# Attention weights kept by key block and multiplied with V once per pair of heads; the memory transposed early, its split parts where the tokens' features were

## The chip, the cores and the metric

The kernel runs on one core of a Trainium2 chip. The metric is the device time of one execution in microseconds (us), the median of several runs. The engines have short names: PE is the matrix engine (PEld its weight loads), DVE the vector engine, ACT the scalar engine, POOL GpSimd, SP the engine whose queue issues most transfers. Each engine works through its own instructions in order.

## The reference

One decoder layer on 512 tokens of 1024 features. What the change touches is the first part, two kinds of attention with 8 heads of 64 features each, and the keys and values of 256 memory tokens:

```
u = rmsnorm(h)
[qA|kA|vA|qB|kB|vB|fA] = u @ w_in
oA = forgetting attention over heads A: softmax(q.k/8 + decay), causal, times v
oB = stick-breaking attention over heads B: exp(log_sigmoid(z) + tail sums), strictly causal, times v
h  = h + concat(rmsnorm(oA), rmsnorm(oB)) @ w_out
h  = h + cross_attention(rmsnorm(h) -> rmsnorm(mem))
h  = h + experts(rmsnorm(h))
out = rmsnorm(h)
```

## The kernel before

All matrix work is in 32-bit floats. Large products are made of three products of split parts (`mm3`, L134): a high part (name ending in `h`) and a rest (ending in `l`), both in the format float32r. A weight unit of 1024 values a partition is loaded by SP (`wload`), copied to its high part by ACT (L89), and its rest is made by DVE (L90). The attention products with V and the transposes are plain float32.

Phase 1 handles the heads in pairs, p = 0 to 3, with one pair of each kind at a time. `qk_proj` makes the queries and keys of a pair (PE rows `pj<-uh,wh`, 512 columns each) and SP copies them into tiles `QQ`, `KH`, `KL`, `QX`, `KX`. `sb_pair` and `fox_pair` are generators that work through three sets of query blocks, BLOCKS = (0), (1, 3), (2), first one head and then the other: products into a PSUM tile (`Z` for stick-breaking, two buffers; `lg` for forgetting attention, one), a chain on DVE and ACT that ends in weights, the transposes of these (`transposed`, L319, rows `tr<-ident,sa` and `tr<-ident,p`), and a copy of the transposes to a tile `pT` (six buffers; by ACT for stick-breaking, by DVE for forgetting attention). When both heads of a set have their `pT`, `av` (L312) multiplies it with V: for each query block i and each key block s from i on, one product of 128 columns for each head. The heads' 64 features go to the upper and the lower half of the partitions of one PSUM tile `o4`, which is to say to two halves of the matrix engine's columns; in the trace each product is two records, 320 for 160 products. `pair_out` (L345) copies a finished `o4` to HO (ACT, L346), squares it (ACT, L351) and adds the squares up (DVE, L352).

The generators run in turn ("sfsf..."). The order in which the instructions then stand on each engine is made when the kernel is built, by a scheduler that moves independent work between them: PE gets the next pair's projections (`pj<-uh`), the values' projections (`pj<-wh,uh`), and in pair 3 the memory's keys (`pj<-mh,wh`) as filling between the steps of the attention.

Before pair 0 the memory is normalised and transposed, and each transpose is split at once by ACT and DVE into `mh` and `ml` (`to_fm`, L131, tiles that live beside the tokens' features `uh` and `ul`). After pair 3 come the rest of the memory's keys and values (rows `pj<-mh,wh`, `pj<-wh,mh`, `lg<-wh,mh`) and then the out projection (first row `pja<-wh,fmh`).

Of the kernel before, what the change touches and what calls it, by code (L numbers as in the profile page):

```python
# [21 lines left out]
S = 512  # L22
D = 1024
NT = 4
# [11 lines left out]
FIRST = 4  # L36


def layer(ctx, tc, a, out, dbg=None):
# [100 lines left out]
    # -------------------------------------------------------------- constants  # L140
# [17 lines left out]
    # ================================================= phase 1: projection, FoX, SB  # L158
# [11 lines left out]
    tuneg = pc.tile([128, 512], F32, name="tuneg")  # L170
    nc.gpsimd.memset(tuneg, -1.0)
    affine(tuneg[:, 384:], [[-1, 128]], OP.is_ge, 0.0, 0, 1)
    one2 = pc.tile([2, S], F32, name="one2")
    nc.gpsimd.memset(one2, 1.0)
# [11 lines left out]
    mp = pool(ckm, "mp", side="left")  # L186
    mh = mp.tile([128, KT, M], F32R, name="mh")
    ml = mp.tile([128, KT, M], F32R, name="ml")
# [13 lines left out]
    # ---- forget gates  # L202
# [20 lines left out]
    # ---- pieces  # L223
# [41 lines left out]
    def qk_proj(g, p):  # L265
# [18 lines left out]
        for hh in range(2):  # L284
# [8 lines left out]
            else:  # L293
# [3 lines left out]
                parts += [(QX, 0, qh[P, :]), (QX, 64, one2), (KX, 0, kl[P, :]),  # L297
# [8 lines left out]
    # what the heads give, by feature: the heads of a pair share a tile  # L306
# [3 lines left out]
    # the tokens come last first: the keys of a query block are its own block and those behind it;  # L310
    # the products of a pair's heads run side by side in the columns of the tensor engine
    def av(o, i, at, pTs, vcol):  # L312
        for s in range(i, NT):
            for hh in range(2):
                nc.tensor.matmul(o[hh * HD:(hh + 1) * HD, i * 128:(i + 1) * 128],  # L315
                                 V[:, s, vcol + hh * HD:vcol + (hh + 1) * HD], pTs[hh][:, at + s - i, :],
                                 start=s == i, stop=s == NT - 1)

    def transposed(p, w, copy):  # L319
        pt = trp.tile([128, NT, 128], F32, name="tr")  # L320
        for s in range(w // 128):
            nc.tensor.transpose(pt[:, s, :], p[:, s * 128:(s + 1) * 128], ident)  # L322
        pT = wk.tile([128, NT, 128], F32, name="pT", bufs=6)
        copy(pT[:, :w // 128, :], pt[:, :w // 128, :])
        return pT

    # blocks of queries that are handled together
# [16 lines left out]
    # the features of a pair of heads go to their place; their squares are summed over the pairs  # L344
    def pair_out(o, g, p):  # L345
# [3 lines left out]
        else:  # L349
            s2 = wk.tile([128, S], F32, name="sa", bufs=5)  # L350
# [3 lines left out]
    def fox_pair(p, ops):  # L354
        o = op_.tile([128, S], F32, name="o4", bufs=2)
        for blocks in BLOCKS:
            at, w = spans(blocks)
            pTs = []
            for Q, K in ops:
# [15 lines left out]
                pTs.append(transposed(p_, w, nc.vector.tensor_copy))  # L375
                if len(pTs) == 1:
                    yield
            for i, cs in at:
                av(o, i, cs.start // 128, pTs, p * 128)
            yield  # L380
        pair_out(o, 0, p)
# [4 lines left out]
    def sb_pair(p, ops):  # L386
        o = op_.tile([128, S], F32, name="o4", bufs=2)
        for blocks in BLOCKS:
            at, w = spans(blocks)
            pTs = []  # L390
            for Q, K in ops:
# [4 lines left out]
                e = wk.tile([128, S], F32, name="sa", bufs=5)  # L396
# [4 lines left out]
                c = wk.tile([128, S], F32, name="sa", bufs=5)  # L401
# [4 lines left out]
                if len(pTs) == 1:  # L406
                    yield
# [60 lines left out]
    for p in range(4):  # L468
# [5 lines left out]
        for c in "sf":  # L474
            for _ in steps[c]:
                pass
# [850 lines left out]
```

## Time and profile before

| | |
|---|---|
| time, median of 3 runs (lowest, highest) | 663.63 us (662.79, 664.0) |
| span of the profiled execution | 662.1 us |
| PE busy, share of the span | 625.6 us, 94% |
| DVE, ACT, POOL busy | 461.6, 376.7, 53.1 us |
| moved by DMA | 128.91 MB, 195 GB/s on average |

The span is the time from the first to the last instruction of the profiled execution; it is 1.5 us below the median. A matmul's duration in the trace includes its way through the array, some 0.17 us in which the next one already runs: what one costs is read from the distance between two starts. Rows by stretch give the stretch and its length, then the busy time (and number of instructions) of PE, PEld, DVE, ACT and POOL, the granted clock of PE as a share of full speed, the share of the DMA engines' time, and GB/s. Rows in order of time give start, duration, engine, line, operation, names and shapes. The trace gives the attention of the four pairs from 68.66 us (the first `Z` product) to 260.07 us (the row behind the last product with V).

### The profile page before, as it was taken

The page shows a single profiled execution, that of the slowest core. Times are in us where ns is not written, and L with a number is a line of the kernel's source. Part 1 is how long each engine was busy: PE and PEld are TensorE (multiplying, and loading weights), DVE is VectorE, ACT ScalarE, POOL GpSimd, SP SyncE. Part 2 cuts the span into 40 slices and gives each one's busy share as a digit, 9 for nine tenths or more (in the row PEclk, how much of TensorE's full clock was granted, in tenths as well). Part 3 has the DMA queues.
Part 4 walks back from the last instruction along what each step waited for, and adds up shares of the span by engine and source line. Part 5 has one row for each costly group of instructions (what it writes and reads, how often), then busy time and mean ns, then how long its engine had stood idle before and what let it go on. Part 6 is the DMA issues. An engine that isn't in the chain of part 4 may idle for free.

```text
span 662.1 us, 10336 instructions
## 1 busy us (share of the span) xinstructions
PE 625.6 (94%) x3595; PEld 507.4 (77%) x3596; DVE 461.6 (70%) x941; ACT 376.7 (57%) x752; POOL 53.1 (8%) x80
## 2 busy tenths in 40 slices
PE   3999999999999999999999999999999999999980
PEld 2988777888877888988888898867767777777750
DVE  4843794963497797855853466347879999989955
ACT  5632556653456676613632354333369898898842
POOL 2000000000000000000000003000152011010350
PEclk9999999999999999999999999999999999999996
DMA  8545744323764634561453223792989999999494
GB/s 279 171 125 133 186 113 116 92 65 92 171 157 107 169 104 152 200 218 35 121 166 96 77 84 88 260 367 99 313 258 366 378 388 380 386 383 385 130 201 174
DMA packets 105497, 128.91 MB, mean 195 GB/s; under 512 B 8456, under 2 KB 82240, under 8 KB 105440
## 3 DMA queue, kind: packets, MB, share of 16 engines
q1 hardware_dynamic: 101120, 114.43, 54.8%
q0 software_dynamic: 4320, 13.77, 7.6%
q8 instruction: 29, 0.48, 0.3%
q14 instruction: 28, 0.23, 0.1%
HBM read 103.96 MB, written 11.56 MB: 174 GB/s over the span
## 4 chain that ended last, share of the span: by engine, by line
PE 82%; DMA 6%; DVE 4%; ACT 3%; issue 2%; POOL 1%; SPq 1%; DVEq 0%; POOLq 0%
PE pj L136 8%; PE pj L138 8%; PE pj L137 8%; PE o L315 5%; PE gu L136 4%; PE pja L136 4%; PE gu L137 4%; PE gu L138 4%; PE pja L137 4%; PE pja L138 4%; PE tr L322 3%; PE tr L129 3%; PE pjb L137 3%; PE pjb L136 3%; PE pjb L138 3%; PE dn L136 2%
## 5 line engine op out<-in xcount | busy, mean ns | idle before, releaser
L90 DVE TENSOR_TENSOR wl<-w,wh 128x1024 fp32r<-128x1024 f32 (+1 forms) x64 | 78.3, 1223 | 81.3 <-ACT wh L89 75.1
L89 ACT CAST wh<-w 128x1024 fp32r<-128x1024 f32 (+1 forms) x64 | 67.2, 1050 | 104.5 <-PE pj L137 37.3
L709 DVE TENSOR_TENSOR wl<-w,wh 128x512 fp32r<-128x512 f32 x168 | 108.5, 686 | 5.5 <-ACT wh L708 5.1
L708 ACT CAST wh<-w 128x512 fp32r<-128x512 f32 x168 | 96.6, 621 | 12.8 <-PE gu L138 9.8
L136 PE MATMUL pj<-uh,wh 128*128 128x512 f32 x128 | 52.1, 407 | 0.0
L138 PE MATMUL pj<-uh,wl 128*128 128x512 f32 x128 | 51.5, 403 | 0.0
L137 PE MATMUL pj<-ul,wh 128*128 128x512 f32 x128 | 51.2, 400 | 0.0
L136 PE MATMUL gu<-wh,xh 128*128 128x512 f32 x120 | 48.5, 404 | 0.2 <-ACT xh L131 0.2
L138 PE MATMUL gu<-wh,xl 128*128 128x512 f32 x120 | 47.6, 397 | 0.0
L137 PE MATMUL gu<-wl,xh 128*128 128x512 f32 x120 | 47.1, 393 | 0.0
L136 PE MATMUL pj<-wh,uh 128*128 128x256 f32 (+1 forms) x128 | 37.7, 294 | 2.3 <-ACT uh L131 2.3
L138 PE MATMUL pj<-wh,ul 128*128 128x256 f32 (+1 forms) x128 | 37.5, 293 | 0.0
L137 PE MATMUL pj<-wl,uh 128*128 128x256 f32 (+1 forms) x128 | 37.3, 292 | 0.0
L315 PE MATMUL o<-pT,V 128*64 128x128 f32 x320 | 33.0, 284 | 0.1
L136 PE MATMUL pja<-wh,fmh 128*128 128x512 f32 x80 | 32.4, 405 | 0.0
L137 PE MATMUL pja<-wl,fmh 128*128 128x512 f32 x80 | 31.9, 399 | 0.0
L138 PE MATMUL pja<-wh,fml 128*128 128x512 f32 x80 | 31.8, 398 | 0.0
L315 PEld LDWEIGHTS o<-pT,V 128*64 128x64 f32 x320 | 21.4, 136 | 10.0 <-issue 5.2
L136 PEld LDWEIGHTS pj<-uh,wh 128*128 128x128 f32 x128 | 24.1, 188 | 6.3 <-issue 1.7
L138 PEld LDWEIGHTS pj<-uh,wl 128*128 128x128 f32 x128 | 24.1, 188 | 5.9 <-issue 0.9
L368 ACT ACTIVATE p<-lg,nm 128x512 f32<-128x512 f32 (+3 forms) x32 | 16.9, 527 | 20.4 <-DVE nm L366 20.3
L137 PEld LDWEIGHTS pj<-ul,wh 128*128 128x128 f32 x128 | 24.1, 188 | 4.8 <-issue 0.3
(356 smaller groups left out, 1633.2 us busy)
## 6 DMA issues: line engine op xcount, KB each, us to landing
w<-in_w_exp_gate_dram SPq DMA_DIRECT2D x64, 256.0 KB, 7.6
w<-in_w_exp_up_dram SPq DMA_DIRECT2D x64, 256.0 KB, 7.6
w<-in_w_exp_down_dram SPq DMA_DIRECT2D x32, 512.0 KB, 7.6
w<-in_w_in_dram SPq DMA_DIRECT2D x24, 512.0 KB, 4.1
w<-in_w_xkv_dram SPq DMA_DIRECT2D x16, 512.0 KB, 4.4
Y<-y SPq DMA_DIRECT2D x14, 512.0 KB, 8.7
KH<-th SPq DMA_DIRECT2D x32, 128.0 KB, 2.3
w<-in_w_out_dram SPq DMA_DIRECT2D x8, 512.0 KB, 4.3
```

Of the source, the lines that this page charges most:

```text
L89: nc.scalar.copy(h, raw)
L90: nc.vector.tensor_sub(l, raw, h)
L129: nc.tensor.transpose(pt[:, j, :], src[:, k * 128:(k + 1) * 128], ident)
L136: nc.tensor.matmul(o, lh, rh, start=start, stop=False)
L137: nc.tensor.matmul(o, lh, rl, start=False, stop=False)
L138: nc.tensor.matmul(o, ll, rh, start=False, stop=stop)
L315: nc.tensor.matmul(o[hh * HD:(hh + 1) * HD, i * 128:(i + 1) * 128], V[:, s, vcol + hh * HD:vcol + (hh + 1) * HD], pTs[hh][:, at + s - i, : ...
L322: nc.tensor.transpose(pt[:, s, :], p[:, s * 128:(s + 1) * 128], ident)
L368: nc.scalar.activation(p_[:, cs], lg[:, cs], AF.Exp, bias=nm, scale=1.0, accum_out=sm)
L708: nc.scalar.copy(h, raw)
L709: nc.vector.tensor_sub(l, raw, h)
```

## The change

- `av` is called once per pair and kind, after all transposes of the pair. It goes through the key blocks, last first, and multiplies each with all query blocks up to it in one product of up to 384 columns for each head: widths 384, 128, 384, 256, 128. A pair's 40 products of 128 columns become 20 (10 for each kind).
- For this the transposed weights of a pair are kept by key block in tiles of 14 blocks, four buffers, which is one pair's need. `transposed` copies to strided places in them.
- `pair_out` of both kinds follows `av`.
- The memory's transposes are copied once, unsplit, to a tile `mT` (ACT one half, DVE the other). `memory()`, called when the last `qk_proj` has been written, splits `mT` into `mh` and `ml` in the place of `uh` and `ul`: four copies on ACT and four subtractions on DVE.
- The two rows of ones in `QX` are written by POOL instead of by transfers from a tile `one2`. `sa` has 4 buffers instead of 5. `vm` gets a pool of its own, which is opened when the attention's tiles are closed.
- Comment lines go. Line numbers of the changed kernel differ: its products with V are L315 too, its transposes L324, its `Z` and `lg` products L346, its `pj` products L137 to L139.

```diff
-                parts += [(QX, 0, qh[P, :]), (QX, 64, one2), (KX, 0, kl[P, :]),
+                nc.gpsimd.memset(QX[64:66, :].bitcast(F32), 1.0)
+                parts += [(QX, 0, qh[P, :]), (KX, 0, kl[P, :]),
...
-    def av(o, i, at, pTs, vcol):
-        for s in range(i, NT):
-            for hh in range(2):
-                nc.tensor.matmul(o[hh * HD:(hh + 1) * HD, i * 128:(i + 1) * 128],
-                                 V[:, s, vcol + hh * HD:vcol + (hh + 1) * HD], pTs[hh][:, at + s - i, :],
-                                 start=s == i, stop=s == NT - 1)
-
-    def transposed(p, w, copy):
+    def av(pTs, vcol):
+        o = op_.tile([128, S], F32, name="o4", bufs=2)
+        runs = [(NT - 1, 0, NT - 1, 3 * NT - 3), (NT - 1, NT - 1, 1, 3 * NT + 1)]
+        runs += [(s, 0, s + 1, 3 * s) for s in range(NT - 2, -1, -1)]
+        for n, (s, i, w, at) in enumerate(runs):
+            for hh in (1, 0):
+                nc.tensor.matmul(o[hh * HD:(hh + 1) * HD, i * 128:(i + w) * 128],
+                                 V[:, s, vcol + hh * HD:vcol + (hh + 1) * HD],
+                                 pTs[hh][:, at:at + w, :],
+                                 start=n == 0, stop=n == len(runs) - 1, skip_group_check=True)
+        return o
+
+    def transposed(p, at, w, pT, copy):
...
-        pT = wk.tile([128, NT, 128], F32, name="pT", bufs=6)
-        copy(pT[:, :w // 128, :], pt[:, :w // 128, :])
-        return pT
+        i = at[0][0]
+        n = w // 128
+        copy(pT[:, 4 * i:4 * i + 3 * n - 2:3, :], pt[:, :n, :])
+
+    def weights_by_key():
+        return [wk.tile([128, 14, 128], F32, name="pT", bufs=PTS) for _ in range(2)]
...
-                pTs.append(transposed(p_, w, nc.vector.tensor_copy))
-                if len(pTs) == 1:
-                    yield
-            for i, cs in at:
-                av(o, i, cs.start // 128, pTs, p * 128)
-            yield
-        pair_out(o, 0, p)
+                transposed(p_, at, w, pTs[hh], nc.vector.tensor_copy)
+                yield
+        W["av0"] = pTs
...
-        to_fm(src, xt, mh, ml, t * 128)
+        for half in range(2):
...
+            (nc.vector.tensor_copy if half else nc.scalar.copy)(
+                mT[:, half * 4:half * 4 + 4, t * 128:(t + 1) * 128], pt)
...
+    def memory():
+        mp = pool(ckm, "mp", side="left")
+        mh, ml = (mp.tile([128, KT, M], F32R, name=n) for n in ("mh", "ml"))
+        for k in range(0, KT, 2):
+            ks = slice(k, k + 2)
+            nc.scalar.copy(mh[:, ks, :], mT[:, ks, :])
+            nc.vector.tensor_sub(ml[:, ks, :], mT[:, ks, :], mh[:, ks, :])
+        return mh, ml
...
+        for g in range(2):
+            pair_out(av(W[f"av{g}"], g * 512 + p * 128), g, p)
...
-    cu.close()
-
+        if p == 2:
+            cu.close()
+            mh, ml = memory()
```

What this does to the order: PE in the kernel before, in the middle of pair 0, where the products with V (`o<-pT,V`; two `o` tiles, one for each kind) stand singly or in sevens between projections and transposes:

```order
L136 MATMUL pj<-uh,wh 128x512
L137 MATMUL pj<-ul,wh 128x512
L138 MATMUL pj<-uh,wl 128x512
L315 MATMUL o_786<-pT,V 64x128 x7
L322 MATMUL tr<-ident,sa 128x128 x4
L136 MATMUL pj<-uh,wh 128x512
L137 MATMUL pj<-ul,wh 128x512
L138 MATMUL pj<-uh,wl 128x512
L136 MATMUL pj<-uh,wh 128x512
L322 MATMUL tr<-ident,p 128x128 x3
L315 MATMUL o_766<-pT,V 64x128
L137 MATMUL pj<-ul,wh 128x512
```

Such groups of products with V stand at 12 places in each pair, 48 in all. PE in the changed kernel, behind the last transposes of pair 0:

```order
L139 MATMUL pj<-wh,ul 128x256
L315 MATMUL o_996<-pT,V 64x384 x2
L315 MATMUL o_996<-pT,V 64x128 x2
L315 MATMUL o_996<-pT,V 64x384 x2
L315 MATMUL o_996<-pT,V 64x256 x2
L315 MATMUL o_996<-pT,V 64x128 x2
L315 MATMUL o_1009<-pT,V 64x384 x2
L315 MATMUL o_1009<-pT,V 64x128 x2
L315 MATMUL o_1009<-pT,V 64x384 x2
L315 MATMUL o_1009<-pT,V 64x256 x2
L315 MATMUL o_1009<-pT,V 64x128 x2
L324 MATMUL tr<-ident,sa 128x128 x4
```

There are four such places, one per pair. In pair 0 and pair 2 they stand behind the first `Z` products of the next pair.

ACT in the kernel before, from pair 2 to pair 3: L346 and L351 copy and square the two `o` tiles of pair 2, L397 begins the chain of pair 3:

```order
L346 COPY HO<-o_1958 128x512
L351 ACTIVATE sa<-o_1958 128x512
L346 COPY HO<-o_1978 128x512
L351 ACTIVATE sa<-o_1978 128x512
L89 CAST wh<-w 128x1024
L279 CAST th<-pj 128x512
L397 ACTIVATE sa<-Z 128x512
```

The same place of ACT in the changed kernel (`th` is the last projection of pair 3, L396 begins its chain):

```order
L273 CAST th<-pj 128x512
L376 ACTIVATE p<-p,rs 128x256
L474 CAST mh<-mT 128x512 x4
L90 CAST wh<-w 128x1024
L351 COPY HO<-o_2132 128x512
L356 ACTIVATE sa<-o_2132 128x512
L351 COPY HO<-o_2147 128x512
L356 ACTIVATE sa<-o_2147 128x512
L396 ACTIVATE sa<-Z 128x512
```

The projection stands ahead now, the four copies of the memory have come in, and the chain of pair 3 still stands behind the copies of the `o` tiles, which here wait for the products with V that PE does after the first `Z` products of pair 3. At the end of pair 3, 99 products of the memory's keys and values stand between the last product with V and the out projection; in the kernel before it was 129, the others are among the attention's steps now.

## Rows read from the trace of the kernel before

**Rows 1.** The page, part 4: the last chain, shares by engine.

```profile
PE 82%; DMA 6%; DVE 4%; ACT 3%; issue 2%; POOL 1%; SPq 1%; DVEq 0%; POOLq 0%
```

**Rows 2.** Busy time by stretch: pairs 0 to 3, then up to out projection.

```profile
68.66:111.50 42.84, 42.34 (x249) 31.42 (x248) 32.46 (x72) 25.89 (x55) 0.00 (x0) 1.00 0.58 145
111.50:177.37 65.87, 65.43 (x442) 55.72 (x440) 39.09 (x78) 32.97 (x67) 0.00 (x0) 1.00 0.40 100
177.37:220.30 42.93, 42.34 (x249) 31.42 (x248) 33.84 (x74) 25.89 (x55) 0.00 (x0) 1.00 0.58 141
220.30:260.07 39.77, 39.09 (x321) 34.53 (x319) 35.71 (x76) 28.25 (x56) 2.09 (x3) 1.00 0.51 139
260.07:276.25 16.18, 16.18 (x139) 16.18 (x139) 13.00 (x27) 12.35 (x21) 0.00 (x0) 1.00 0.51 172
```

**Rows 3.** PE in order of time, pair 0: start, duration, instruction.

```profile
82.28 0.39 PE L137 MATMUL pj<-ul,wh 128*128 128x512 f32 x1
82.51 0.40 PE L138 MATMUL pj<-uh,wl 128*128 128x512 f32 x1
82.84 1.09 PE L315 MATMUL o<-pT,V 128*64 128x128 f32 x14
83.86 0.50 PE L136 MATMUL pj<-uh,wh 128*128 128x512 f32 x1
84.19 0.39 PE L137 MATMUL pj<-ul,wh 128*128 128x512 f32 x1
```

**Rows 4.** The same in pair 3: one product with V, then transposes.

```profile
240.32 0.28 PE L136 MATMUL pj<-mh,wh 128*128 128x256 f32 x1
240.57 0.43 PE L315 MATMUL o<-pT,V 128*64 128x128 f32 x2
240.94 0.38 PE L137 MATMUL pj<-ml,wh 128*128 128x256 f32 x1
241.16 0.28 PE L138 MATMUL pj<-mh,wl 128*128 128x256 f32 x1
...
242.46 0.28 PE L137 MATMUL pj<-ml,wh 128*128 128x256 f32 x1
242.57 0.49 PE L322 MATMUL tr<-ident,p 128*128 128x128 f32 x3
242.82 0.36 PE L138 MATMUL pj<-mh,wl 128*128 128x256 f32 x1
243.02 0.28 PE L136 MATMUL pj<-mh,wh 128*128 128x256 f32 x1
```

**Rows 5.** Writers of o: durations (ns, least/median/most), first and last start.

```profile
L315 PE MATMUL o<-pT,V x320: 272/273/324, 76.1 to 259.9; 128*64 128x128 f32 x160
```

**Rows 6.** Plain float32, 512 columns: the line; two in order of time.

```profile
L1249 PE MATMUL dn<-w,hf x32: 590/592/596, 488.7 to 636.2; 128*128 128x512 f32 x32
...
568.70 1.02 PE L1249 MATMUL dn<-w,hf 128*128 128x512 f32 x2
```

**Rows 7.** Busy time from the first DVE step of pairs 0 and 3.

```profile
69.39:101.70 32.31, 31.81 (x195) 24.05 (x194) 29.78 (x67) 20.18 (x44) 0.00 (x0) 1.00 0.58 149
220.97:258.90 37.93, 37.24 (x307) 33.10 (x306) 34.86 (x75) 26.52 (x55) 2.09 (x3) 1.00 0.49 134
```

**Rows 8.** Pair 3 in order of time: ACT's first step, DVE's last copy.

```profile
221.70 0.60 ACT L397 ACTIVATE sa<-Z 128x512 f32<-128x512 f32 x1
...
258.76 0.42 DVE L324 COPY pT<-tr 128x256 f32<-128x256 f32 x1 [1.22 <-PE tr L322]
```

**Rows 9.** PE's waits over the whole span: total us, times, longest.

```profile
PE tr L322 <- DVE sa L404: 1.4, 3, 0.6
```

**Rows 10.** Groups in the attention (busy us, mean ns): squares, their sums.

```profile
L351 ACT ACTIVATE sa<-o 128x512 f32<-128x512 f32 x6 | 3.6, 603 | 0.0
L352 DVE TENSOR_TENSOR sq<-sq,sa 128x512 f32<-128x512 f32 x6 | 4.1, 691 | 2.8 <-ACT sa L351 2.8
```

**Rows 11.** Two of the memory's four splits on DVE, as in rows 5.

```profile
L131 DVE TENSOR_TENSOR ml<-o,mh x2: 680/680/681, 46.1 to 46.7; 128x512 fp32r<-128x512 f32 x2
```

More of the change, by code (lines that the diff above doesn't have):

```diff
@@ L36 @@
 FIRST = 4
+PTS = 4
 def layer(ctx, tc, a, out, dbg=None):
@@ L169, in layer @@
     affine(negs, [[1, 128]], OP.is_gt, NEG, 0, -1)
[L170 to L174, printed above, removed]
+    mT = pc.tile([128, KT, M], F32, name="mT")
     vp = pool(c1, "vp", side="right")
@@ L185, in layer @@
     ckm = ExitStack()
-    mp = pool(ckm, "mp", side="left")
-    mh = mp.tile([128, KT, M], F32R, name="mh")
-    ml = mp.tile([128, KT, M], F32R, name="ml")
     cu = ExitStack()
@@ L349, in pair_out @@
         else:
-            s2 = wk.tile([128, S], F32, name="sa", bufs=5)
+            s2 = wk.tile([128, S], F32, name="sa", bufs=4)
             nc.scalar.activation(s2, o, AF.Square)
@@ L354, in fox_pair @@
     def fox_pair(p, ops):
-        o = op_.tile([128, S], F32, name="o4", bufs=2)
+        pTs = weights_by_key()
         for blocks in BLOCKS:
             at, w = spans(blocks)
-            pTs = []
-            for Q, K in ops:
+            for hh, (Q, K) in enumerate(ops):
                 lg = lgp.tile([128, S], F32, name="lg", bufs=1)
@@ L386, in sb_pair @@
     def sb_pair(p, ops):
-        o = op_.tile([128, S], F32, name="o4", bufs=2)
+        pTs = weights_by_key()
         for blocks in BLOCKS:
             at, w = spans(blocks)
-            pTs = []
-            for Q, K in ops:
+            for hh, (Q, K) in enumerate(ops):
                 z = zp.tile([128, S], F32, name="Z", bufs=2)
@@ L395, in sb_pair @@
                     nc.vector.tensor_add(z[:, cs.start:cs.start + 128], z[:, cs.start:cs.start + 128], negs)
-                e = wk.tile([128, S], F32, name="sa", bufs=5)
+                e = wk.tile([128, S], F32, name="sa", bufs=4)
                 nc.scalar.activation(e[:, :w], z[:, :w], AF.Abs)
@@ L400, in sb_pair @@
                 nc.vector.scalar_tensor_tensor(e[:, :w], z[:, :w], 0.0, e[:, :w], op0=OP.max, op1=OP.add)
-                c = wk.tile([128, S], F32, name="sa", bufs=5)
+                c = wk.tile([128, S], F32, name="sa", bufs=4)
                 for i, cs in at:
@@ L404, in sb_pair @@
                 nc.vector.tensor_sub(c[:, :w], z[:, :w], c[:, :w])
-                pTs.append(transposed(c, w, exp))
-                if len(pTs) == 1:
-                    yield
-            for i, cs in at:
-                av(o, i, cs.start // 128, pTs, 512 + p * 128)
-            yield
-        pair_out(o, 1, p)
+                transposed(c, at, w, pTs[hh], exp)
+                yield
+        W["av1"] = pTs
     cn = ExitStack()
     nw = pool(cn, "nw", side="right")
+    tuneg = nw.tile([128, 512], F32, name="tuneg", bufs=1)
+    nc.gpsimd.memset(tuneg, -1.0)
+    affine(tuneg[:, 384:], [[-1, 128]], OP.is_ge, 0.0, 0, 1)
     src = three()
@@ L460, in layer @@
         rms(nw, xt, g_mem, xt, D)
-        to_fm(src, xt, mh, ml, t * 128)
-    cn.close()
-    qk = pool(c1, "qk", side="right")
-    wk = pool(c1, "wk", side="right")
+        for half in range(2):
+            pt = next(src)
+            for j in range(4):
+                k = half * 4 + j
+                nc.tensor.transpose(pt[:, j, :], xt[:, k * 128:(k + 1) * 128], ident)
+            (nc.vector.tensor_copy if half else nc.scalar.copy)(
+                mT[:, half * 4:half * 4 + 4, t * 128:(t + 1) * 128], pt)
+    cn.close()
+    def memory():
[6 more added lines that the diff above has]
+        return mh, ml
+    ca = ExitStack()
+    qk = pool(ca, "qk", side="right")
+    wk = pool(ca, "wk", side="right")
     mark("qk0")
@@ L490, in layer @@
     kl_ = kmp.tile([128, KT, M], F32R, name="kml")
-    vm = [kmp.tile([128, 2, D], F32R, name=n) for n in ("vmh", "vml")]
     for j2 in range(4):
@@ L502, in layer @@
         nc.vector.tensor_sub(kl_[:, sl, :], kps, kh_[:, sl, :])
+    ca.close()
+    vmp = pool(ckm, "vmp", side="left")
+    vm = [vmp.tile([128, 2, D], F32R, name=n) for n in ("vmh", "vml")]
     def xv_weights(c):
```

## Prediction

> **What bounds the kernel now.** I read the page first: PE holds 82% of the chain that ended last [rows 1]. Then the stretches from one pair's first `Z` product to the next one's: PE is busy in all but half a microsecond to a microsecond of each, at full clock, while DVE is busy 32.5 of 42.8 us in pair 0, 39.1 of 65.9 in pair 1, 33.8 of 42.9 in pair 2, 35.7 of 39.8 in pair 3 [rows 2]. PE's only wait there of any size is 1.4 us in three places [rows 9]. So PE sets the time of the attention, and DVE is not far behind it in pairs 0, 2 and 3. A busy PE is not PE at its peak, so I then looked at the starts in order of time.
>
> **What a group of products with V costs on PE.** Projections of 512 columns start 0.23 us apart (82.28, 82.51). From 82.51 to 84.19, with a group of products with V between them, it is 1.68 us [rows 3]. Two projections are 0.46 of that, so the group takes 1.22 us. What of it is work? A record of plain float32 with 512 columns takes 0.43 us (two last 1.02 us together and 0.592 each, so the second starts 0.43 after the first) [rows 6], which is 0.107 us for 128 columns. Two heads side by side share that, 0.0535 us a record: 14 records are 0.75 us. 0.47 us are left over. A single product (two records) takes 241.16 − 240.32 less two projections of 256 columns at 0.12, 0.60 us, for 0.11 of work at the paired rate: 0.49 left over, of which 0.11 is that its partner is missing [rows 4]. Three transposes between projections, plain float32 as well, take 243.02 − 242.46 − 0.24 = 0.32 us, and that is three times 0.107: nothing left over [rows 4]. So it is not the change of number format that costs, but going over to the halves of the columns and back. I take 0.45 us for each group; many stand beside transposes and share nothing else with them, so I bound it by 0.40 and 0.49.
>
> **The sum for PE.** The 320 records run from 76.1 to 259.9 us [rows 5], in 48 groups, 12 per pair; four groups are left. 44 × 0.45 = 19.8 us go (17.6 to 21.6 by the bounds). The work in the groups stays: a pair has 80 records of 128 columns, 80 × 0.0535 = 4.3 us, and the wider products cover the same columns. It moves, though, and so do 30 memory products of 0.12 us (3.5 us) from behind pair 3 into it. By stretch, with the times of rows 2:
> pair 0: 42.84 − 12 × 0.45 − 4.3 (its products with V now come in pair 1) = 33.1;
> pair 1: 65.87 − 5.4 + 2 × 0.45 + 4.3 = 65.7;
> pair 2: 42.93 − 5.4 − 4.3 = 33.2;
> pair 3: 39.77 − 5.4 + 0.9 + 4.3 + 3.5 = 43.1;
> to the out projection: 16.18 − 3.5 = 12.7.
> Together 187.8 us in place of 207.6.
>
> **What is late next.** The steps that DVE and ACT do are the same, and PE had given them 0.45 us of slack 12 times per pair. In pair 0, DVE did what pair 1's first `Z` products must wait for (both buffers of `Z`) in 32.3 us, busy 29.8 [rows 7]; PE now comes to 33.1. The two queues are about equally long and wait for each other at every step. If PE loses the share that DVE idled there (8%), it is 35.9; if PE stays ahead, 33.1. I take +1.2 us, in pair 2 too: nearer to no wait, since DVE was 92% busy in this stretch while PE hardly waited. In pair 1 PE has 65.7 us against 39 of DVE; only the step from the last copy to the products with V is new there: +0.3.
>
> In pair 3 it is worse. ACT's chain for pair 3 stands behind the copies of pair 2's `o` tiles, and these wait for products with V that now stand behind pair 3's first `Z`: four `Z` products (0.9), two transposes (0.2), one projection (0.1), the products with V (4.3 + 0.45), then copy and square of the second tile, 0.60 each [rows 10]: 7.2 us after the first `Z` instead of 1.4 (221.70 − 220.30) [rows 2, 8]. DVE's work from there on is that of before (34.9 us from 220.97 [rows 7], less some 2.5 that is done ahead of it: two small steps on `Z`, a projection's rest of the size of rows 11, a weight split of twice that; an estimate), plus two sums of squares at 0.69 [rows 10] and one key split of about 0.7: 34.5 us. It can begin with the sums of squares, about 5.8 us after the first `Z`. Without a gap the last copy is at 40.3, and with 4.8 for the products with V the stretch takes 45.1; with the gaps of before (37.93 for 34.86 [rows 7]) it is 48.1. Both are above PE's 43.1. I take 47.0: +3.9 us. At the end the sums over the squares come 16 products (1.9 us) after the last product with V, and copy, square and sum take 1.9 [rows 10], with hand-overs: +0.3.
>
> Waits added: 1.2 + 0.3 + 1.2 + 3.9 + 0.3 = 6.9 us, with ends of 0 and 14. Forecast: 19.8 − 6.9 = 12.9 us less. The span of 662.1 would become 649.2; it lies 1.5 us below the median, which I leave as it is: 663.6 − 12.9 = **650.7 us**.
>
> **Edits that I cost at nothing.** The memory's early copies: four splits each on ACT and DVE, 0.68 us on DVE [rows 11], become two copies each, near 46 us, where PE has projections to do; no gain. `memory()` puts four subtractions of 0.68 before pair 3 on DVE; they lie under the 4.3 us of products with V. Without that cover they would add up to 2.7 us to pair 3. Eight small transfers of ones leave SP's queue, and POOL, all but idle in the attention [rows 2], writes the rows instead; PE had no wait on them. SP's order is otherwise that of before but for weight loads moved by a few places, and DMA is at 0.40 to 0.58 there [rows 2]. The copies of transposes go to places three blocks apart, in pieces of 128 values: I take the duration of before, 0.42 us for two blocks [rows 8]; a tenth more would be 1 us on DVE over 24 copies, inside the ends of the waits. What lies behind 276 us moves up as a whole: its loads start when tiles of the stages before come free, and these come free earlier by as much.
>
> **The rivals.**
> PE alone sets the pace and no wait is added: 663.6 − 19.8 = 643.8. For it: DVE reached 92% busy in pair 0 under a PE that barely waited. Against it: pair 3's late chain.
> DVE and ACT set it in every pair: 35.9 in pairs 0 and 2 (+2.8 each), +1 in pair 1, 49 in pair 3 (+6), 1 at the end, 13.6 us in all: 657.4. For it: 76 to 79% busy in pairs 0 and 2 becomes over 90% of the shorter time.
> The wide products pair badly. If the four records of two neighbouring products start in the order in which they are written (upper first and second, lower first and second), an upper second record runs beside a lower first one, and a lower second one beside the next run's first. With equal widths that costs nothing, and the 14 records of rows 3 fit it as well as any other pairing. With widths 384, 128, 384, 256, 128 unequal ones meet: 640 columns more per `o` tile, at 0.43 us for 512 [rows 6] 0.54 us, eight times 4.3 us: 655.0. The Trainium skill, page "TensorE: Matmul & The Clock Gate", Part 3 (the list of what overlaps), speaks for this and so against the change: matmuls start and end in program order, and only weight loads are pulled ahead. No row here decides it, since all widths are equal.
> The wide products do not run side by side at all: each record then takes its full 0.107 us per 128 columns, 80 × 0.107 = 8.6 us per pair in place of 4.3. Four pairs cost 17.2 us more, and the change loses: 667.9, slower than before. It decides from the point where 12.9 is used up, three quarters of the pairs' overlap gone. Against it: halves and their order are as before, and records of rows 3 do overlap.
> The change doesn't do what it says: if the 0.47 us of rows 3 were the hand-over of each `pT` copy and not the halves of the columns, one late hand-over per pair and kind would remain and DVE's waits would come on top: about 662. Against it: transposes also wait for hand-overs and show nothing left over [rows 4].
>
> **How the numbers follow.** Forecast 0.45 (its own range 647 to 654.5); PE alone 0.17; DVE and ACT everywhere 0.25; bad pairing 0.06; no overlap 0.03; not what it says 0.04. The predicted time is 650.7. The range of 8 in 10 goes from PE alone to DVE and ACT everywhere, with a little for their own spread: 643.5 to 658.0. Below it lies a group cost of 0.49 with no wait, above it the last two rivals. About 0.2% (1.3 us) is what a measurement of this kernel can tell from no change. The first four cases are faster by more; of the fifth and sixth, 0.03 is slower, and the rest is split between the same and the slower side: faster 0.93, same 0.03, slower 0.04.
>
> **What would show it.** In the changed profile: 160 records of L315 in four groups, each some 4.3 us long plus 0.45 (8.6 if nothing overlaps, 5.4 if the pairing is bad); pairs 0 and 2 from first `Z` to first `Z` in 33 to 36 us; PE waiting for DVE or ACT, in pair 3 above all, some 4 us between its first `Z` and its last product with V; the stretch from the last product with V to the out projection in 13 us; everything behind it as long as before. Wrong would make it: PE waits of over 14 us in the attention, or groups of L315 twice as long.

## The result, and the profile after

The changed kernel takes 653.65 us (median of 4 runs, 653.4 to 654.53) where the kernel before takes 663.65 (662.79 to 664.0): ratio 0.985, 95% interval 0.983 to 0.987, 10.0 us less. The prediction was 650.7, its range 643.5 to 658.0. The profiled execution took 653.75 us, with a span of 652.1.

The page's part 4, which answers [rows 1]: PE's share of the chain that ended last has fallen, those of DVE, DMA and ACT have grown.

```profile
PE 75%; DVE 8%; DMA 7%; ACT 5%; issue 2%; POOL 1%; SPq 0%; DVEq 0%; ACTq 0%; POOLq 0%
```

Busy time by stretch, pairs 0 to 3 and then up to the out projection, as in [rows 2]:

```profile
68.44:102.13 33.69, 33.08 (x167) 26.12 (x166) 31.21 (x71) 22.73 (x49) 1.04 (x2) 1.00 0.61 149
102.13:169.23 67.10, 65.83 (x443) 55.63 (x442) 39.49 (x80) 35.08 (x73) 1.04 (x2) 1.00 0.45 115
169.23:202.98 33.75, 33.04 (x168) 26.10 (x167) 31.22 (x71) 22.74 (x49) 1.04 (x2) 1.00 0.63 149
202.98:251.38 48.40, 44.91 (x353) 38.13 (x351) 42.96 (x87) 34.48 (x68) 2.09 (x3) 1.00 0.54 153
251.38:264.10 12.72, 12.72 (x109) 12.68 (x108) 9.37 (x22) 10.24 (x18) 0.00 (x0) 1.00 0.50 155
```

Pairs 0 and 2 are 9.2 us shorter each, pair 1 is 1.2 longer, pair 3 8.6 longer (two pairs' products with V lie in each of these, and 30 more of the memory's products in pair 3), the tail 3.5 shorter. Together 195.66 us in place of 207.59: 11.9 less.

The writers of `o`, as in [rows 5], and one of their four groups on PE in order of time, as in [rows 3]:

```profile
L315 PE MATMUL o<-pT,V x160: 272/379/537, 104.7 to 251.2; 128*64 128x384 f32 x64, 128*64 128x128 f32 x64, 128*64 128x256 f32 x32
```

```profile
104.45 0.28 PE L138 MATMUL pj<-wl,uh 128*128 128x256 f32 x1
104.66 4.54 PE L315 MATMUL o<-pT,V 128*64 128x384 f32 x40
109.13 0.66 PE L324 MATMUL tr<-ident,sa 128*128 128x128 f32 x4
```

From 104.45 to 109.13 are 4.68 us, less 0.12 for the projection 4.56. Of these 80 × 0.0545 = 4.36 us are work at the paired rate, so the wide products do run side by side.

PE's waits over the attention (us in total, times, longest). In the kernel before they are the row of 1.4 us in [rows 9] and one of 0.2 us:

```profile
PE tr L324 <- DVE sa L403: 2.0, 5, 0.7
PE tr L324 <- ACT p L376: 1.4, 2, 1.2
PE Z L346 <- DVE sa L403: 1.2, 3, 0.6
PE pj L139 <- DVE wl L91: 0.7, 1, 0.7
```

Behind the attention the profiled execution needed 387.97 us to its end, before it was 385.90: 2.07 us were lost there, and not in a stage that the change touches. Up to the last gathers nothing is lost. The gathers of `Y` then took 17.1 us from the first to the last (start of each), before 16.2, and from the last one's start to the end it is 24.8 us, before 23.3.

```profile
L1293 POOL DMA_INDIRECT HO<-Y,slot x8: 1541/1609/2016, 610.1 to 627.2; - x8
```

The same line in two kernels further below: the first has the changed attention and one small edit, the second the attention of before.

```profile
L1293 POOL DMA_INDIRECT HO<-Y,slot x8: 1533/1616/2015, 611.2 to 627.6; - x8
```

```profile
L1288 POOL DMA_INDIRECT HO<-Y,slot x8: 1542/1618/2007, 624.1 to 641.2; - x8
```

16.4 us with the change, 17.1 without it. From the out projection to the end the profiled executions of this study took, with the same work there, 385.9 and 386.5 us in the two kernels with the attention of before, and 385.4 to 389.6 us in the twelve with the changed one. The 2.07 us lie within what these kernels differ by; whether the change has a part in them is not shown.

### The profile page after: what moved, and what is told of

Read it like the earlier page. It is cut to its first block, busy times and chain, and to the rows that moved or that the text cites. A ratio compares the mean times of both kernels' runs of the same rounds, so it can differ in the third digit from the quotient of the medians.

```text
span 652.1 us, 10038 instructions
## 1 busy us (share of the span) xinstructions
PE 609.8 (94%) x3435; PEld 496.6 (76%) x3436; DVE 460.8 (71%) x943; ACT 375.6 (58%) x754; POOL 56.8 (9%) x87
## 4 chain that ended last, share of the span: by engine, by line
PE 75%; DVE 8%; DMA 7%; ACT 5%; issue 2%; POOL 1%; SPq 0%; DVEq 0%; ACTq 0%; POOLq 0%
PE pj L137 6%; PE pj L139 6%; PE pj L138 6%; PE gu L137 4%; PE pja L137 4%; PE gu L138 4%; PE gu L139 4%; PE pja L138 4%; PE pja L139 4%; PE tr L130 3%; PE pjb L138 3%; PE pjb L137 3%; PE pjb L139 3%; PE o L315 2%; PE dn L137 2%
## 5 line engine op out<-in xcount | busy, mean ns | idle before, releaser
L90 ACT CAST wh<-w 128x1024 fp32r<-128x1024 f32 (+1 forms) x64 | 67.2, 1050 | 101.4 <-PE pj L138 33.1
L137 PE MATMUL pj<-uh,wh 128*128 128x512 f32 x128 | 51.3, 401 | 0.0
L139 PE MATMUL pj<-uh,wl 128*128 128x512 f32 x128 | 51.2, 400 | 0.0
L137 PE MATMUL gu<-wh,xh 128*128 128x512 f32 x120 | 48.5, 404 | 0.2 <-ACT xh L132 0.2
L139 PE MATMUL gu<-wh,xl 128*128 128x512 f32 x120 | 47.6, 397 | 0.0
L137 PE MATMUL pj<-wh,uh 128*128 128x256 f32 (+1 forms) x128 | 37.5, 293 | 2.2 <-ACT uh L132 2.2
L139 PE MATMUL pj<-wh,ul 128*128 128x256 f32 (+1 forms) x128 | 37.5, 293 | 0.0
L137 PE MATMUL pja<-wh,fmh 128*128 128x512 f32 x80 | 32.5, 406 | 0.0
L139 PE MATMUL pja<-wh,fml 128*128 128x512 f32 x80 | 31.8, 397 | 0.0
L137 PEld LDWEIGHTS pj<-uh,wh 128*128 128x128 f32 x128 | 24.1, 188 | 5.1 <-issue 0.2
L372 ACT ACTIVATE p<-lg,nm 128x512 f32<-128x512 f32 (+3 forms) x32 | 16.9, 527 | 19.0 <-DVE nm L370 18.7
L139 PEld LDWEIGHTS pj<-uh,wl 128*128 128x128 f32 x128 | 24.1, 188 | 4.8
L137 PEld LDWEIGHTS pj<-wh,uh 128*128 128x128 f32 x128 | 25.1, 196 | 3.0 <-ACT uh L132 2.8
L139 PEld LDWEIGHTS gu<-wh,xl 128*128 128x128 f32 x120 | 22.5, 188 | 5.3 <-issue 0.2
```

The lines of the kernel that those rows point to most:

```text
L90: nc.scalar.copy(h, raw)
L137: nc.tensor.matmul(o, lh, rh, start=start, stop=False)
L139: nc.tensor.matmul(o, ll, rh, start=False, stop=stop)
L372: nc.scalar.activation(p_[:, cs], lg[:, cs], AF.Exp, bias=nm, scale=1.0, accum_out=sm)
```

## The experiments

Times of other runs are set against runs of the kernel before on the same chip (medians of 663.7 to 664.5 us).

### What a group costs: two twins

```diff
         ps = pj.tile([128, S], F32, name="pj")
+        nc.tensor.matmul(ps[0:64, 0:128], ident[:, 0:64], ident, start=True, stop=True)
```

The same line stands ahead of each value projection; the twin has 128 in place of both 64.

> The changed kernel with 32 extra products of plain float32, 128 columns each, which use half of the matrix engine's columns; one stands ahead of each of the 16 query and key projections and of the 16 value projections, and its result is overwritten, so nothing is left out. Theory (going over to the halves of the columns and back costs PE about 0.4 us, whatever stands around it): the single product of rows 4 took 0.60 us, so 32 of them take up to 19 us, and this kernel stands 12 to 14 us above its twin whose extra products use all columns. Rival (what was left over in the groups of the kernel before was the hand-over of the weights' copies): these products wait for nothing, so the two twins are equal and both stand some 7 us (32 x 0.21) above 653.7. Products that fall where PE isn't the bound cost less in both; the distance between starts on PE tells the price by itself.

> The twin: the same 32 extra products, plain float32, 128 columns each, but over all of the matrix engine's columns. Theory: only their own work, 2 records of 0.107 us each, 6.8 us at the most: about 660, and from start to start 0.21 us for each. Rival (the change of number format between float32r and plain float32 costs the 0.4 us): as high as the other twin, 667 to 673.

Measured: 664.15 us with half of the columns, 657.70 with all of them. PE in order of time, first half, then all:

```profile
55.17 0.40 PE L139 MATMUL pj<-uh,wl 128*128 128x512 f32 x1
55.50 0.43 PE L266 MATMUL pj<-ident 128*64 128x128 f32 x2
55.86 0.50 PE L137 MATMUL pj<-uh,wh 128*128 128x512 f32 x1
56.20 0.39 PE L138 MATMUL pj<-ul,wh 128*128 128x512 f32 x1
```

```profile
52.57 0.40 PE L139 MATMUL pj<-uh,wl 128*128 128x512 f32 x1
52.81 0.38 PE L266 MATMUL pj<-ident 128*128 128x128 f32 x2
52.95 0.48 PE L137 MATMUL pj<-uh,wh 128*128 128x512 f32 x1
53.27 0.39 PE L138 MATMUL pj<-ul,wh 128*128 128x512 f32 x1
```

From the projection ahead to the second one behind it is 1.03 us and 0.70 us. Less two projections (0.46) the product costs 0.57 over half of the columns and 0.24 over all; 0.22 are its own work. At every other place between two projections of 512 columns it is the same, 1.02 to 1.03 us and 0.68 to 0.70. So going over to the half and back costs some 0.33 us, without any hand-over in sight, and plain float32 over all columns costs next to nothing beyond its work. The rival falls. Of the expected 12 to 14 us between the twins 6.5 appeared: the price is 0.33 and not 0.40 or more, and in pairs 0 and 2 it is hidden. These two pairs take 34.7 us with the half columns and 34.5 with all of them, where four products at 0.33 should make 1.3 us of difference. So at that length PE alone no longer sets the time there.

What of the 0.45 us that I read in [rows 3, 4] is more than 0.33 is the missing partner: all 48 groups of the kernel before have an odd number of products, one of them without its neighbour (0.11 us). In [rows 3], 14 records are seven products.

### The same groups, narrow products

```diff
+        runs = [(s, i + j, 1, at + j) for s, i, w, at in runs for j in range(w)]
```

> The changed kernel with every product with V cut into products of 128 columns: 40 per pair instead of 20, in the same four groups. Theory (the number of groups made the gain, the number and width of products did not): 653.7 within 1 us, groups 4.6 to 5 us long as before, from 80 records. Rival (the gain came from half as many records, 19.8 us over 160 records, 0.124 us each): back at about 663 to 670, groups of about 10 us.

Measured: 657.00 us (ratio 0.990, 0.988 to 0.993). Neither came, because the groups did not stay: a product of one block waits for fewer copies, and the scheduler puts some of them ahead. The trace has 320 records in 20 groups. One of them, PE in order of time:

```profile
98.30 0.38 PE L325 MATMUL tr<-ident,sa 128*128 128x128 f32 x2
98.61 0.44 PE L316 MATMUL o<-pT,V 128*64 128x128 f32 x4
98.98 0.49 PE L139 MATMUL pj<-uh,wl 128*128 128x512 f32 x1
99.31 0.40 PE L137 MATMUL pj<-uh,wh 128*128 128x512 f32 x1
```

The attention with its tail takes 201.9 us, 6.3 more than in the changed kernel: 0.39 us for each of 16 more groups. The lower clock in pair 3 (0.96 over 43.8 us) can have cost up to 1.8 us of it, which would leave 0.28 for each. The records are those of the kernel before again, and most of the gain is still there. That speaks for the number of groups and against the number of records, but less cleanly than it was meant to.

### One head after the other

```diff
-        for n, (s, i, w, at) in enumerate(runs):
-            for hh in (1, 0):
+        for hh in (1, 0):
+            for n, (s, i, w, at) in enumerate(runs):
```

> The changed kernel with the loops of the products with V exchanged: all of one head's products of a kind, then all of the other's, so that two halves of the columns are never neighbours but once. Theory (two heads' products run side by side when they are neighbours): the groups grow from 4.7 to about 8.6 to 9.1 us, four times 4 us, and the time goes to 666 to 671, slower than the kernel before. Rival (the engine's time on the products does not depend on neighbours, or other waits hide it): 653.7 to 657.

Measured: 663.49 us, no gain left against the kernel before (ratio 1.000, 0.998 to 1.001). The group of pair 0 on PE:

```profile
104.05 0.28 PE L138 MATMUL pj<-wl,uh 128*128 128x256 f32 x1
104.26 7.07 PE L315 MATMUL o<-pT,V 128*64 128x384 f32 x40
111.26 0.44 PE L324 MATMUL tr<-ident,sa 128*128 128x128 f32 x2
```

104.05 to 111.26 less 0.12 is 7.09 us, 2.5 more than in the changed kernel, and four times that is about the 9.8 us by which the kernel is slower. So the neighbourhood of the two heads carries as much as the whole change brings. It is less than the 4 us per group that I expected; why is told at the end.

### The memory's part alone

Before, with `mT`, `memory()` and the later pool of `vm`, and nothing else of the change (diff above).

> The kernel before with the memory's part of the change alone: transposes copied once to mT, split by four copies on ACT and four subtractions on DVE after the last query and key projection, the pool of vm opened later. Products with V stay in 48 groups. Theory of the prediction (this part costs nothing): 663.6 within 1.3 us. Rival (what it adds to DVE and ACT at the start of pair 3, 2.5 and 2.2 us, has no cover here, since there are no 4.5 us of products with V in a row over it): up to 666.3.

Measured: 667.61 us, ratio 1.005 (1.003 to 1.006): 3.2 us slower, the rival. Pairs 0 to 2 take their old times to 0.03 us. Pair 3 and the tail:

```profile
219.41:262.92 43.51, 41.36 (x330) 35.88 (x328) 38.71 (x81) 30.62 (x60) 2.09 (x3) 1.00 0.46 131
262.92:278.02 15.10, 15.10 (x129) 15.10 (x129) 12.73 (x26) 11.55 (x20) 0.00 (x0) 1.00 0.56 176
```

58.61 us against 55.95 in [rows 2], 2.7 more. PE behind the first `Z` products of pair 3:

```profile
220.11 0.39 PE L339 MATMUL Z<-KL,QQ 128*128 128x512 f32 x1
221.48 0.39 PE L136 MATMUL pj<-mh,wh 128*128 128x256 f32 x1 [0.98 <-ACT mh L473]
222.34 0.38 PE L136 MATMUL pj<-mh,wh 128*128 128x256 f32 x1 [0.47 <-DVE tl L278]
222.94 0.38 PE L137 MATMUL pj<-ml,wh 128*128 128x256 f32 x1 [0.21 <-DVE ml L474]
```

The memory's products are PE's filling here, and they now wait for the splits. The length is the 2.7 us that the prediction named for the case without cover, but by another way: it had put it on DVE's four subtractions, and the longest of these waits is for ACT's copies.

### What sets pair 3: rests and sums on POOL

```diff
-            nc.vector.tensor_sub(ml[:, ks, :], mT[:, ks, :], mh[:, ks, :])
+            nc.gpsimd.tensor_sub(ml[:, ks, :], mT[:, ks, :], mh[:, ks, :])
```

> The changed kernel with the memory's four subtractions (L475, 2.5 us on DVE) on POOL. They stand at 205.25 to 207.74 us, under the products with V, ahead of pair 3's work on DVE. Theory (they are covered there, as the prediction had it): no gain, and the products of the memory wait a little for POOL if it is slower; 653.5 to 655. Rival (they delay pair 3's chain as they did when the memory's part was put into the kernel before alone): the stretch of pair 3 falls by 1.5 to 2.5 us.

```diff
-            nc.vector.tensor_add(sq[g], sq[g], s2)
+            nc.gpsimd.tensor_add(sq[g], sq[g], s2)
```

> The changed kernel with the six sums of squares (L357, 0.69 us each) on POOL instead of DVE. Two of them stand at the head of DVE's work in pair 3 (209.89 and 211.57). Theory (in pair 3 DVE is the limit from its first step on): the stretch of pair 3 is 1.0 to 1.5 us shorter, the rest as it was, 652 to 652.7; the sum after the last product with V may lose some of it again if POOL is slower than DVE there. Rival (DVE has room, the late start alone counts): 653.7, or some tenths more.

Measured: 653.15 us (ratio 0.982, 0.980 to 0.985) and 654.79 us (0.985, 0.982 to 0.988), neither told apart from the changed kernel. Pair 3 takes 48.88 and 48.56 us. In the changed kernel the four subtractions are covered, as predicted: behind them DVE waits 1.02 us for ACT in any case. The three sums less on DVE in this stretch (its busy time falls from 42.96 to 41.13 us) gain nothing, but this does not speak against my theory that DVE is the limit there. Two of them stand ahead of the step with which DVE takes up ACT's first results of pair 3's chain (L399, 213.51). Without these sums DVE waits there instead, for PE and for ACT (1.27 us, where it was 0.66):

```profile
210.84 0.30 DVE L368 TENSOR_TENSOR lg<-lg,negc 128x128 f32<-128x128 f32 x1 [1.19 <-PE lg L346]
213.14 0.16 DVE L374 RECIPROCAL rs<-sm 128x1 f32<-128x1 f32 x1 [1.27 <-ACT p L372]
```

The third (250.45) stands behind the last copy of transposes. PE's order is that of the changed kernel in the first run and almost that in the second.

The chain of waits of the changed kernel in pair 3 (start, us, what) runs over DVE and ACT up to 228, and then:

```profile
228.63 3.93 DMA w<-in_w_xkv_dram
...
232.66 1.05 ACT wh L90
233.71 0.57 ACT p L372 x2
...
237.96 3.47 DMA w<-in_w_xkv_dram
...
241.50 1.05 ACT wh L90
242.55 0.42 ACT p L376
```

Two loads of the memory's weights are on it. ACT's casts of these units stand in its order ahead of steps of the attention (`p`, L372 and L376), and these wait with them. ACT waited 3.5 us for loads in pair 3; in the kernel before none. With the sums on POOL the same two loads are on the chain (228.86 and 238.38).

A place on the chain does not yet tell what its removal is worth. Here is the stretch from the step at 213.51 to the end of the last copy of transposes, and the same stretch in the kernel with one head after the other, whose DVE and ACT have the same order:

```profile
213.51:246.62 33.11, 30.11 (x239) 28.39 (x238) 32.29 (x69) 23.11 (x48) 2.09 (x3) 1.00 0.42 120
220.58:253.62 33.04, 30.10 (x239) 28.37 (x238) 32.33 (x69) 23.09 (x48) 2.09 (x3) 1.00 0.33 101
```

DVE is busy 32.29 of 33.11 us. As long as it has this work to do there, nothing else, the loads included, can have cost more than 0.8 us of the stretch. In the second kernel a group of products with V takes 2.5 us longer, DVE's step comes 13.06 us after the first `Z` product of pair 3 instead of 10.53, and the last copy ends 46.10 us after it instead of 43.64. So a later start moves the end by as much. The late start and DVE's queue behind it, added up, are the length of pair 3.

### Without the loads, with a fourth place for them, with a later copy

```diff
-            h, l = wget(kmaj(w_xkv, slice(j * 128, j * 128 + 128)), [KT, 128])
+            if j == 0:
+                raw = wload([kmaj(w_xkv, slice(0, 128))], [KT, 128])
+            h, l = wsplit(raw, [KT, 128])
```

> The changed kernel with one of the eight weight units of the memory's keys loaded and split eight times, so that seven loads of 512 KB are left out and the keys are those of one unit; all splits and products are still done. In the chain of waits of the changed kernel two loads stand on the path of pair 3 (228.6 to 232.6 and 238.0 to 241.5 us), and ACT, in whose order the casts of the weights stand between the steps of the attention, waits 3.5 us for them. Theory (the weights' loads set the end of pair 3): its stretch falls from 48.4 to 44.5 to 46.5 us, the time by 2 to 4 us. Rival (DVE's queue, busy 35.1 of 36.7 us from 209.9 on, sets it, and the waits for loads are inside its time): the stretch stays within 1 us of 48.4.

```diff
-    ring(w=[(wp, 3)], wh=[(wp, 3)], wl=[(wp, 3)])
+    ring(w=[(wp, 3), (vp, 1)], wh=[(wp, 3)], wl=[(wp, 3)])
```

> The changed kernel with four places for loaded weight units in the first phase instead of three (half of the memory's transposes wait in the place where pair 3's features go, which makes the room), so that loads start one unit earlier; nothing is left out. Theory (the weights' loads set the end of pair 3): ACT no longer waits for them there, the stretch of pair 3 is 1.5 to 3.5 us shorter, 650 to 652.5. Rival (DVE's queue sets it): 653 to 654.5.

```diff
+            if n == 1 and p:
+                for g in range(2):
+                    pair_out(outs[g], g, p - 1)
...
-        for g in range(2):
-            pair_out(av(W[f"av{g}"], g * 512 + p * 128), g, p)
+        outs = [av(W[f"av{g}"], g * 512 + p * 128) for g in range(2)]
```

> The changed kernel with the copies and squares of a pair's two o tiles written behind the next pair's first stick-breaking and first forgetting step instead of ahead of them; nothing is left out. In the trace of the changed kernel ACT begins pair 3's chain (L396) 8.0 us after the first Z product (210.94 - 202.98), behind the copies and squares, and DVE is then busy nearly without a gap to the last weights' copy at 246.2. Theory (this late start makes pair 3's stretch 48.4 us long): the chain starts some 6 us earlier, PE's own 43 us become the limit, the stretch falls to 43 to 46 us and the time to 648.5 to 651.5. Rival (the weights of the memory's projections, which land late at 232.7 and 241.5, or DVE's load itself, set the end): 653 to 654.

The fourth has these copies and the sums on POOL:

> The changed kernel with both edits, the o tiles' copies behind the next pair's first steps and the sums of squares on POOL. Theory (late start and DVE's load are one limit, the length of DVE's queue in pair 3): PE is the limit in pair 3, and what is left to gain is bounded by PE alone; 647.5 to 650.5, at most 1 us below the kernel with the late copies alone. Rival (neither is the limit): 653 to 654.

The fifth has four places and, in the memory's keys, every second rest on POOL:

```diff
+            h, l = wsplit(wload([kmaj(w_xkv, slice(j * 128, j * 128 + 128))], [KT, 128]), [KT, 128],
+                          nc.gpsimd if j % 2 else nc.vector)
```

> The kernel with four places for loaded weight units, and besides the rests (L91, 1.21 us each on DVE) of every second of the memory keys' eight weight units on POOL, which POOL would do in about 3 us each (estimate from the memory's four subtractions of half that size, 5.98 us there); nothing is left out. Taking away 1.4 us of DVE's work alone, the late start alone, and the waits for loads alone each left pair 3 and the tail together within a microsecond or longer. Theory (two limits of nearly one length stand side by side in pair 3, DVE's queue and the loads with what hangs on them, so that only both edits together gain): pair 3 and the tail together fall from 61.1 to 57 to 59.5 us, the time to 650 to 652.5. Rival (the order in which the engines' steps stand, each waiting for the other by turns, sets the length, not one engine's work): 60.5 to 62.5 us for both, 653.5 to 656.

Measured, with times of pair 3 from its first `Z` product; the last column is DVE from its first step L399 of pair 3 to the end of the last copy of transposes, as above:

| | us | ratio | pair 3 + tail | ACT's first step | last copy | DVE busy, of stretch |
|---|---|---|---|---|---|---|
| before | 663.65 | | 55.95 | 1.4 | 38.5 | 32.8 of 35.5 |
| changed | 653.65 | 0.985 | 61.12 | 8.0 | 43.2 | 32.3 of 33.1 |
| one load for eight | 655.48 | 0.986 | 61.84 | 9.6 | 45.0 | 32.2 of 33.2 |
| four places | 654.98 | 0.985 | 61.51 | 8.1 | 45.3 | 33.7 of 35.0 |
| later copies | 655.97 | 0.986 | 64.08 | 5.8 | 45.6 | 35.4 of 38.2 |
| later copies, sums on POOL | 655.07 | 0.986 | 62.03 | 4.4 | 43.4 | 34.4 of 37.4 |
| four places, rests on POOL | 660.57 | 0.994 | 65.72 | 7.8 | 50.1 | 36.1 of 40.2 |

In each of these the scheduler made another order of PE, DVE and ACT, so none changes one thing alone. None of the theories' times (647.5 to 652.5 us) came. Without loads, and with four places, ACT no longer waits for a load there and no load of these weights is on the chain; but DVE's stretch is as full as in the changed kernel, and pair 3 with the tail is no shorter:

```profile
215.36:248.55 33.19, 31.70 (x243) 29.04 (x241) 32.23 (x70) 24.16 (x49) 2.09 (x3) 1.00 0.14 38
```

So the theory of the loads falls. The row is that of one load for eight, whose pair 3 is 1.6 us longer, at 50.0, because its chain starts 1.7 us later. With the later copies the chain of pair 3 starts 2.1 and 3.5 us earlier, not 6 (the memory's splits and a cast stand ahead of it now). But DVE then has 3.1 and 2.1 us more to do before the last copy and waits 2.8 and 3.0 us in between, and the end does not move forward. An earlier start alone is therefore not enough in these orders; what it would bring with DVE's work unchanged was not run.

The last run was to remove two limits at once, and did not: two of DVE's steps took 2.1 us longer each while POOL made rests (below). That is as much as the 4.2 us that pair 3 and the tail are longer than with four places alone. What is shown is that in the changed kernel's own order DVE's queue, behind a late start, sets the length of pair 3 to within 0.8 us. Which order would let pair 3 run at PE's pace stays open.

## Why the prediction was right

By the prediction's own steps, in us:

| stretch | PE alone | with waits, forecast | measured |
|---|---|---|---|
| pair 0 | 33.1 | 34.3 | 33.69 |
| pair 1 | 65.7 | 66.0 | 67.10 |
| pair 2 | 33.2 | 34.4 | 33.75 |
| pair 3 | 43.1 | 47.0 | 48.40 |
| tail | 12.7 | 13.0 | 12.72 |
| sum | 187.8 | 194.7 | 195.66 |

- **The group's price** (0.45 us, 44 groups, 19.8 us) held, with another make-up: 0.33 for the halves of the columns and back, 0.11 for a product without its partner. Pairs 0 and 2 give a lower bound: each is 9.2 us shorter, 4.4 of that are the products that moved, and the rest is 0.40 for each of 12 groups if no wait was added. The changed kernel's groups have no product without a partner; each leaves 0.2 us over and a first product behind it that delays its successor (142.82 to 143.05 where 0.12 is usual), 0.3 us together. The Trainium skill, page "TensorEngine Tiling (Array Packing)", Key Properties, says that a change of tiling mode, not of the tile alone, drains the engine. The twins agree that such a change costs time, 0.33 us for going there and back.
- **The waits** are 7.9 us in place of 6.9. In pairs 0 and 2 half of what I took came (0.6 of 1.2 each), near the lower end. In pair 1 it is 1.4 in place of 0.3: the second set of `Z` products behind pair 0's products with V waits 0.6 us for DVE (`sa`, L403), and two transposes wait for the same step, 0.6 together; I had looked there for one hand-over only. In pair 3 it is 5.3 in place of 3.9, the term that was sized worst.
- **The mechanism in pair 3** is the one that the prediction has: a late start, DVE's queue nearly without a gap, then the products with V. Measured are 6.9 + 36.7 + 4.8 = 48.4 us (DVE busy 35.1 of the 36.7). The prediction had 5.8 for the start, 34.5 to 37.5 for DVE (without gaps and with those of before) and 4.8. So most of the 1.4 us that were missing is the start: PE comes to pair 2's products with V 2.4 us after the first `Z` product, not 1.2. The loads of the memory's weights, which I costed at nothing ("moved by a few places"), stand on the chain twice, but leaving seven of them out did not shorten DVE's stretch.
- **The memory's part** costs nothing in the changed kernel, by the run with POOL, as written. Without the cover it costs the 2.7 us that were written, but the longest wait is for ACT's copies and not for DVE's subtractions, so that the number is in part right by luck.
- **What lies behind** took 2.07 us more in the profiled execution, by which the gain came out 10.0 and not 12. I had let it move up as a whole, at no cost. It varies by 4.2 us between kernels that have the same work there; the cause stays open.
- **The rivals.** PE alone (643.8): the waits are there. DVE and ACT everywhere (657.4): pairs 0 and 2 are 33.7, not 35.9, but pair 3 lies near its 49. Bad pairing (groups of 5.4 us): the group takes 4.56. No overlap (667.9): not so, and with one head written after the other, which leaves part of the overlap, it costs 9.8 us. The change doesn't do what it says (662): the twins show the price without any hand-over.

## What to carry to other kernels

Read the price of a small group from starts to starts, and take two twins that differ in one property to say what the price is for. When the engine that sets the pace loses its idle places, add up the others in each stretch: those that had a tenth of slack become the limit, and the gain ends there. A step that costs nothing under cover can cost its full length elsewhere. And a chain of waits names what ended last at each step, not what its removal is worth: two loads stood on it, and without them nothing was gained, because DVE's queue beside them was full. Before a step is moved to POOL to relieve DVE, look whether DVE's steps beside it keep their length.

## What the runs showed of the hardware

**Two heads overlap even when they are written apart.** With one head after the other the 80 records at 0.109 us per 128 columns would take 8.7 us and took 7.09. The starts in the trace tell why: a first record of 256 columns (the upper head's fourth product) starts at 105.820, and at 105.826 one of 384 starts, which is the lower head's first product; the upper head's fifth, of 128 columns, is written ahead of it and starts at 106.252. The same pattern stands twice more in this group, at 107.391 and 108.956. So a product of the other half can start before one that is written ahead of it, if PE holds them in the order in which they are written; the order in the built program is not on record for this run. The Trainium skill, page "TensorE: Matmul & The Clock Gate", Part 3, The mechanism, has it that matmuls are strictly in program order at start and end. For products of different column halves these starts, under the same condition, say otherwise. The bad pairing, which the prediction drew from that rule, did not come.

**A wait of PE can be paid twice.** In the last run PE waited 2.44 us for DVE (to 231.23) and 2.40 us (to 242.10) in pair 3. Its granted clock by stretch is the third number from the end; 0.50 is the level of 1.2 GHz, 1.00 that of 2.4. The row by itself is from the run with narrow products, behind a wait of 1.11 us (to 212.81):

```profile
229.00:231.00 2.00, 0.00 (x0) 0.00 (x0) 2.00 (x3) 0.00 (x0) 1.03 (x1) 1.00 0.00 0
235.00:238.00 3.00, 3.00 (x28) 3.00 (x27) 3.00 (x7) 2.94 (x7) 0.37 (x1) 1.00 0.01 2
240.00:242.00 2.00, 0.00 (x0) 0.00 (x0) 2.00 (x4) 0.47 (x1) 0.76 (x1) 1.00 0.06 9
242.00:243.50 1.50, 1.40 (x12) 1.37 (x13) 1.47 (x5) 0.74 (x2) 0.00 (x0) 0.99 0.96 324
243.50:246.90 3.40, 3.40 (x18) 3.40 (x18) 2.25 (x6) 1.69 (x6) 2.09 (x3) 0.50 0.24 34
246.90:248.00 1.10, 1.10 (x11) 1.10 (x10) 0.81 (x2) 0.23 (x1) 0.00 (x0) 1.00 0.94 315
```

```profile
214.90:218.30 3.40, 3.40 (x16) 3.21 (x15) 1.96 (x3) 2.01 (x3) 0.00 (x0) 0.50 0.63 142
```

Behind the second wait PE went on at full clock and was then at the lower level for 3.4 us, which costs PE up to 1.7 us more (an estimate: half of it). Behind the first wait, as long, the clock stayed at 1.00; behind the shorter one of the other run it fell. So the length of a single wait does not tell whether the clock falls. In the changed kernel, whose longest wait in the attention is 1.2 us, it stays at 1.00 in every stretch.

**Steps of DVE can stand still while POOL subtracts.** Both long waits of PE have this behind them. A scan of 128 columns (L402) takes 0.41 us in the changed kernel; in the last run the two of pair 3 took 2.53 us each (mean of one, the number ahead of the second bar), first in the changed kernel, then in the last run:

```profile
L402 DVE TENSOR_TENSOR_SCAN sa<-sa 128x128 f32<-128x128 f32 x2 | 0.8, 406 | 0.0
L402 DVE TENSOR_TENSOR_SCAN sa<-sa 128x128 f32<-128x128 f32 x2 | 5.1, 2530 | 0.0
...
237.63 3.13 POOL L91 TENSOR_TENSOR wl<-w,wh 128x1024 fp32r<-128x1024 f32 x1 [7.61 <-ACT wh L90]
238.50 2.54 DVE L402 TENSOR_TENSOR_SCAN sa<-sa 128x128 f32<-128x128 f32 x1
```

Each began while POOL made a rest and ended 0.28 us behind it (241.04 and 240.76 here). The run with the memory's subtractions on POOL has a sum of squares that took 1.77 us instead of 0.69 in the same way (210.08). Other steps kept their length beside POOL, such as L403 at 217.24 with 0.69 us. What sets the two kinds apart was not tested.
